# The last plain column group of an output projection in two parts, one ahead of seven products and one behind them

## The chip, the cores and the metric

The kernel runs on one core of a Trainium2 chip. The metric is device time in microseconds (us), the median of three runs. Engines are named as the profile names them: PE (TensorE matmul), PEld (its weight load), DVE (VectorE), ACT (ScalarE), POOL (GpSimd), SP (the engine that issues most DMAs; "SPq" is its queue). POOL issues DMAs of its own on a second queue.

## The reference

One encoder layer: 16 meta tokens and 512 real ones, width 2048, float32. Only the end matters here: two mixers of 1024 columns each are gated, put side by side and projected once; the result is normalised by row and added to the input.

```
ya = gqa_axial_mixer(...)  * silu(ga)        # mixer A, 8 heads of 128
yb = diff_attn_mixer(...)  * silu(gb)        # mixer B, 8 heads of 128
y  = concatenate([ya, yb]) @ w_out           # (tokens, 2048) x (2048, 2048)
h  = h + rmsnorm(y, post_norm_g)             # mean square over the 2048 columns
return h[:, N_META:, :]                      # 512 rows
```

The kernel splits every operand into a high part (rounded to float32r) and a low part (the rest), and multiplies in three matmuls: high x high, low x high, high x low.

## The kernel before, in words

**Rows, columns, contraction.** The output has four row blocks of 128 tokens (`t` = 0..3) and four column groups of 512 (`g` = 0..3). The contraction runs over 16 head blocks `j` of 128; the weights are laid out so that 0..7 are mixer B and 8..15 mixer A. `oh[j]`, `ol[j]` are the high and low parts of a head block; the unsplit heads lie in DRAM as `oscr`.

**Plain groups.** `dense_out(g)` computes one column group for all four row blocks: 16 head blocks x 4 row blocks x 3 matmuls = 192 matmuls of 128x512, into four PSUM banks.

**Seven products.** Groups 1 and 2 are computed together by a Strassen-like scheme over halves (row halves x contraction halves x the two groups): seven `product` calls of 48 matmuls in the place of eight. Two operands of the calls are sums: of weight blocks, kept in four tiles `ch0`..`ch3` ("chain") that are changed between calls, and of heads, `t1`..`t4`, each four pairs of high and low tiles. `u` tiles hold two of these in turn, `v` tiles the other two. A head sum is made from halves of `oscr` loaded into tiles `ts`, a DVE subtraction, the high part by ACT (`hi`, line 306) and the low part by DVE (`lo`, line 309).

**Weight blocks.** Weights of 128x1024 (two head blocks by 512 columns, 512 KB) pass through a list `todo` in the order of use. `fetch` keeps two ahead: DMA into `st` (3 buffers, SP queue, line 147), `wh` by ACT (line 154), `wl` by DVE (line 155), 3 buffers each. Numbered from the start of the projection, blocks 1 to 8 serve group 0 and 9 to 16 group 3; then each product takes four. A plain group's block feeds 24 matmuls, a product's 12. For chain blocks there is no `st`: `wh` and `wl` are split from `ch`.

**Order before.** Group 0, group 3 (whole), then products 1 to 7: heads B lower rows, heads A lower rows, t1, t2, heads A upper rows, t3, t4. Chain sums are made in part by a DMA that adds (on the POOL queue), in part by a load into `st` and a DVE addition (line 700). During group 3 `first_sums` loads three half heads per step and makes t1 and t2; `third_sum` and `fourth_sum` stand in products 4 and 6. Row blocks 2 and 3 are finished ahead of product 7; product 7 does its last three weight blocks row block by row block, and `end` finishes row blocks 0 and 1.

**What sets the order.** Within one engine instructions run in the order that the tile framework's scheduler gave them when the kernel was built, from its own model of durations; it moves loads and splits far ahead of where they stand in the code. Each engine and each DMA queue then waits in order: an instruction whose input is late holds up all behind it.

Of the kernel before, what the change touches and what calls it, by code (L numbers as in the profile page):

```python
# [10 lines left out]
F32 = mybir.dt.float32  # L11
# [97 lines left out]
def kernel(ctx: ExitStack, tc: tile.TileContext, xT, xn, xm, w_s, w_t, w_q, w_o,  # L109
# [581 lines left out]
    def summed(add=None, fresh=None):  # L691

        def step(i):
# [3 lines left out]
            if add:  # L697
# [9 lines left out]
    todo += whole(0) + whole(3) + plain(0, 0) + plain(0, 1) + summed((0, 0)) + summed((0, 1))  # L707
    todo += summed((1, 0), fresh=(0, 0)) + summed() + plain(1, 1)
# [57 lines left out]
    def dense_out(g, pool, beside=None):  # L766

        pss = [pool.tile([P, 512], F32, name="po", tag="pd") for _ in range(TT)]
        for j0 in range(0, KT, 2):
            wh, wl = fetch()  # L770
            for j in (j0, j0 + 1):
# [5 lines left out]
                c = slice((j - j0) * 512, (j - j0 + 1) * 512)  # L777
                for t in range(TT):
                    tq = slice(t * P, (t + 1) * P)
                    mm(pss[t], oh[j][:, tq], wh[:, c], start=(j == 0), stop=False)  # L780
                    mm(pss[t], ol[j][:, tq], wh[:, c], start=False, stop=False)
                    mm(pss[t], oh[j][:, tq], wl[:, c], start=False, stop=(j == KT - 1))
                    lanes.poll()
            if beside:
                beside(j0 // 2)
        return pss

    first = dense_out(0, pd)
# [9 lines left out]
    def heads_of(i, half, dma):  # L798

        t = yp.tile([P, 2, NP], F32, name="ts", tag="ts", bufs=6)  # L800
        dma.dma_start(out=t, in_=oscr[i].rearrange("i p q -> p i q")[:, :, half])
        return t
# [10 lines left out]
    t1, t2, t3, t4 = [], [], [], []  # L813

    def first_sums(i):
        b0, b1, a1 = [heads_of(j, half, nc.gpsimd)
                      for j, half in ((i, lo_), (i, hi_), (4 + i, hi_))]
        TTv(out=b0, in0=b1, in1=b0, op=SUB)
        t1.append(operand("u", i, b0))
        TTv(out=a1, in0=a1, in1=b0, op=SUB)  # L820
        t2.append(operand("v", i, a1))

    def first_chain(i):
        nc.gpsimd.dma_start(out=chain[i], in_=block(1, 0, i))
        nc.gpsimd.dma_start(out=chain[i], in_=block(1, 1, i), accum_op=ALU.add)

    def third_sum(i):
        b1, a1 = heads_of(i, hi_, nc.sync), heads_of(4 + i, hi_, nc.sync)
        TTv(out=a1, in0=a1, in1=b1, op=SUB)
        t3.append(operand("u", i, a1))  # L830

    def fourth_sum(i):
        a0 = heads_of(4 + i, lo_, nc.sync)
        TTv(out=a0, in0=t2[i][0].bitcast(F32), in1=a0, op=SUB)
        TTv(out=a0, in0=a0, in1=t2[i][1].bitcast(F32), op=ALU.add)
        t4.append(operand("v", i, a0))
# [7 lines left out]
    def square(t, g, src):  # L844
        jk = yp.tile([P, 512], F32, name="jko", tag="jko", bufs=1)
        at = (0, 1, 3, 2)[g]
        nc.scalar.activation(jk, src, AF.Square, accum_out=ssy[t][:, at:at + 1])
# [6 lines left out]
    def product(ops, pool, beside=None, done=None):  # L854
# [184 lines left out]
```

## Time and profile before

| | |
|---|---|
| median of 3 runs | 955.04 us (954.67 to 955.67) |
| the profiled execution's own time | 955.66 us |
| its span, first to last instruction | 953.9 us |
| mean granted TensorE clock | 0.99 of full |
| group 0 ends, group 3 ends, product 7 starts, last matmul starts | about 810, 854.7, 922.67, 940.65 us |

All times below are in the span of that one execution. In a row of a timeline the columns are start, duration, engine, line, operation, output and inputs, count, and in brackets how long the engine had been idle and what ended that wait. A DMA row's last number is the median time from issue to landing.

### The profile page before, as it was taken

To read this page: it belongs to the slowest core of one execution; us is meant where nothing else is said; L and a number is where in the kernel's file an instruction comes from. 1 tells how busy PE (TensorE), PEld (TensorE's weight loads), DVE (VectorE), ACT (ScalarE), POOL (GpSimd) and SP (SyncE) were. 2 spreads that over 40 slices of the span, in tenths; PEclk is the share of its full clock that TensorE was granted. 3 is DMA by queue.
4 is the path that set the end of the run, shared out by engine and by line. 5 is a ranking of instruction groups with operands and counts; after the bars stand their busy time and mean duration, and the time that the engine had idled before them with its cause. 6 is when DMAs were issued, how large, how long until landed. Compare 5 with 4: busy or idle time off the path is not lost.

```text
span 953.9 us, 14190 instructions
## 1 busy us (share of the span) xinstructions
PE 926.4 (97%) x5498; PEld 810.8 (85%) x5498; DVE 584.6 (61%) x974; ACT 482.0 (51%) x845; POOL 164.0 (17%) x250
## 2 busy tenths in 40 slices
PE   9999999999999999999999999998999999999983
PEld 8899898989989898998997888886888888888862
DVE  6386576757575574757554274447554662476996
ACT  6664655546464554746552254354555743245531
POOL 0001010101001010101201041226212123201054
PEclk9999999999999999999999999999999999999996
DMA  9742122222223222312223223211222346976785
GB/s 333 260 159 99 67 88 88 79 77 100 76 78 99 82 84 77 100 67 78 89 67 100 89 68 109 67 58 54 80 75 78 128 141 202 292 226 193 232 278 196
DMA packets 40611, 117.16 MB, mean 123 GB/s; under 512 B 4672, under 2 KB 9536, under 8 KB 40416
## 3 DMA queue, kind: packets, MB, share of 16 engines
q1 hardware_dynamic: 37072, 104.71, 33.2%
q0 software_dynamic: 3328, 11.54, 4.1%
q8 instruction: 43, 0.70, 0.3%
q14 instruction: 24, 0.20, 0.1%
q10 hardware_dynamic: 144, 0.01, 0.0%
HBM read 107.85 MB, written 8.39 MB: 122 GB/s over the span
## 4 chain that ended last, share of the span: by engine, by line
PE 84%; DVE 7%; DMA 2%; POOL 2%; ACT 2%; issue 1%; SPq 0%; DVEq 0%; POOLq 0%; ACTq 0%
PE pd L63 54%; PE po L63 14%; PE sc L63 6%; PE pv L63 5%; PE tr L66 5%; DVE wl L155 1%; DVE qn L578 1%; DMA st<-in_w_o_dram 1%; DVE y L939 1%; POOL qn L592 1%; DMA ch<-in_w_o_dram 1%; POOL ssh L241 1%; DMA xns<-in_xn_dram 1%; DMA xs<-in_xT_dram 1%; ACT qn L650 0%
## 5 line engine op out<-in xcount | busy, mean ns | idle before, releaser
L63 PE MATMUL pd<-xh,wh 128*128 128x264 f32 (+1 forms) x992 | 333.3, 336 | 0.0
L63 PE MATMUL pd<-xl,wh 128*128 128x264 f32 (+1 forms) x992 | 324.9, 327 | 0.4 <-DVE xl L180 0.4
L63 PE MATMUL pd<-xh,wl 128*128 128x264 f32 (+1 forms) x992 | 324.9, 328 | 0.4 <-DVE wl L155 0.4
L154 ACT ACTIVATE wh<-st 128x1024 fp32r<-128x1024 f32 (+2 forms) x135 | 139.8, 1038 | 208.3 <-PE pd L63 90.5
L155 DVE TENSOR_TENSOR wl<-st,wh 128x1024 fp32r<-128x1024 f32 (+2 forms) x135 | 161.7, 1198 | 98.9 <-ACT wh L154 97.7
L63 PEld LDWEIGHTS pd<-xh,wl 128*128 128x128 f32 x992 | 186.6, 188 | 17.8 <-DVE wl L155 0.7
L63 PEld LDWEIGHTS pd<-xh,wh 128*128 128x128 f32 x992 | 187.3, 189 | 12.9 <-ACT xh L179 0.2
L63 PEld LDWEIGHTS pd<-xl,wh 128*128 128x128 f32 x992 | 187.5, 189 | 12.0 <-DVE xl L180 0.6
L63 PE MATMUL po<-wh,ol 128*128 128x512 f32 x176 | 69.6, 396 | 0.9 <-DVE ol L309 0.9
L63 PE MATMUL po<-wh,oh 128*128 128x512 f32 x176 | 70.3, 400 | 0.0
L63 PE MATMUL po<-wl,oh 128*128 128x512 f32 x176 | 69.8, 397 | 0.0
L463 ACT ACTIVATE p<-p,mx 128x528 f32<-128x528 f32 x64 | 46.5, 728 | 34.2 <-POOL mx L460 34.0
L453 DVE CUSTOM_DVE_ANT_0 p<-sc,dist 128x528 f32<-128x528 f32 x64 | 44.9, 702 | 24.0 <-PE sc L63 23.5
L309 DVE TENSOR_TENSOR pl<-tr,ph 128x512 fp32r<-128x512 f32 x64 | 43.4, 688 | 16.2 <-ACT ph L306 15.0
L306 ACT ACTIVATE ph<-tr 128x512 fp32r<-128x512 f32 x64 | 37.6, 590 | 30.9 <-PE tr L66 30.6
L63 PE MATMUL pd<-wh,xh 128*128 128x512 f32 x128 | 52.2, 408 | 0.8 <-DVE vf L300 0.8
L66 PE MATMUL tr<-ident,p 128*128 128x128 f32 (+1 forms) x320 | 50.9, 273 | 1.7 <-DVE gA L558 0.9
L63 PE MATMUL pd<-wh,xl 128*128 128x512 f32 x128 | 50.6, 395 | 0.0
L63 PE MATMUL pd<-wl,xh 128*128 128x512 f32 x128 | 50.5, 395 | 0.0
L66 PEld LDWEIGHTS tr<-ident,p 128*128 128x128 f32 (+1 forms) x320 | 37.3, 132 | 13.4 <-DVE gA L558 1.6
L413 POOL TENSOR_SCALAR pm<-pm 32x256 fp32r<-32x256 f32 x32 | 20.1, 627 | 149.7 <-ACT pm L306 145.8
L460 POOL TENSOR_SCALAR mx<-mx 128x2 f32<-128x2 f32 x32 | 12.1, 377 | 196.0 <-DVE mx L453 196.0
(206 smaller groups left out, 1582.6 us busy)
## 6 DMA issues: line engine op xcount, KB each, us to landing
st<-in_w_t_dram SPq DMA_DIRECT2D x82, 512.0 KB, 3.6
st<-in_w_o_dram SPq DMA_DIRECT2D x40, 512.0 KB, 4.3
st<-in_w_q_dram SPq DMA_DIRECT2D x16, 512.0 KB, 3.6
xs<-in_xT_dram SPq DMA_DIRECT2D x16, 264.0 KB, 5.7
xns<-in_xn_dram SPq DMA_DIRECT2D x8, 512.0 KB, 5.3
ch<-in_w_o_dram POOLq DMA_DIRECT2D x8, 512.0 KB, 8.8
out_dram<-y SPq DMA_DIRECT2D x16, 256.0 KB, 2.3
os<-oscr SPq DMA_DIRECT2D x6, 512.0 KB, 3.6
```

Source lines behind the costliest of these rows:

```text
L63: self._add(self.nc.tensor.matmul(out, lhsT, rhs, start=start, stop=stop), us)
L66: self._add(self.nc.tensor.transpose(out, in_, ident), 0.109)
L154: nc.scalar.activation(wh[:, c], st[:, c], AF.Copy)
L155: nc.vector.tensor_tensor(out=wl[:, c], in0=st[:, c], in1=wh[:, c].bitcast(F32), op=ALU.subtract)
L241: nc.gpsimd.tensor_tensor(out=dst, in0=dst, in1=mhalf[:rows, :dst.shape[1]], op=ALU.pow)
L306: nc.scalar.activation(dst, src, AF.Copy)
L309: nc.vector.tensor_tensor(out=dst, in0=src, in1=h.bitcast(F32), op=ALU.subtract)
L413: nc.gpsimd.tensor_scalar(out=pm[32:64], in0=pm[0:32].bitcast(F32), scalar1=1.0, scalar2=1.0, op0=ALU.mult, op1=ALU.mult)
L453: nc.vector.tensor_tensor_reduce(out=two(p), in0=sc[:, :, :HALF], in1=two(dist[:, w0:w0 + NT]), scale=1.0, scalar=-3.0e38, op0=ALU.add, op ...
L460: nc.gpsimd.tensor_scalar(out=mx, in0=mx, scalar1=-0.125, scalar2=1.0, op0=ALU.mult, op1=ALU.mult)
L463: nc.scalar.activation(p2[m], p2[m], AF.Exp, scale=0.125, bias=mx[:, m:m + 1], accum_out=sm[:, m:m + 1])
L578: nc.vector.scalar_tensor_tensor(out=raw[:, i, :], in0=raw[:, i, :], scalar=ss[:rows, i:i + 1], in1=g[:rows], op0=ALU.mult, op1=ALU.mult)
```

## The change

Group 3 is cut by contraction: its mixer B half (head blocks 0..7, weight blocks 9 to 12) runs where the whole group ran, its mixer A half (96 matmuls, four weight blocks) runs behind the seven products, in the same four PSUM banks, which stay taken in between. The last three blocks of that half go row block by row block, and `finish` ends each of the four row blocks as it comes. The products are now heads B lower (blocks 13 to 16), heads A lower (17 to 20), t1, t2, heads A upper, t4, t3. The first and second head sums are made apart: `first_sum` in the B half of group 3, `second_sum` in product 1, `fourth_sum` in product 5, `third_sum` in product 6. The tiles `ts` go from 6 buffers to 2, beside 4 new ones named `r` that keep an unsplit sum for the second one. One of the three additions to the chain is moved from DVE to a DMA that adds, on the POOL queue.

```
-            if add:
+                nc.gpsimd.dma_start(out=chain[i], in_=block(*add, i), accum_op=ALU.add)
+            elif add:
...
-    todo += whole(0) + whole(3) + plain(0, 0) + plain(0, 1) + summed((0, 0)) + summed((0, 1))
-    todo += summed((1, 0), fresh=(0, 0)) + summed() + plain(1, 1)
+    todo += whole(0) + whole(3)[:4] + plain(0, 0) + plain(0, 1) + summed((0, 0)) + summed((0, 1))
+    todo += summed((1, 0), fresh=(0, 0)) + plain(1, 1) + summed() + whole(3)[4:]
...
+    def dense_out(g, pss, first=0, end=KT, tail=0, done=None, beside=None):
...
+        last = [fetch(len(todo)) for _ in range(tail // 2)] if tail else []
+        for t in range(TT):
+            for j in range(end - tail, end):
+                part(t, j, last[(j - end + tail) // 2])
+            if done:
+                done(t, pss[t])
...
+    def first_sum(i):
+        b0 = heads_of(i, lo_, nc.gpsimd, "r", 4)
+        b1 = heads_of(i, hi_, nc.gpsimd)
+        nc.gpsimd.dma_start(out=chain[i], in_=block(1, 0, i))
+        nc.gpsimd.dma_start(out=chain[i], in_=block(1, 1, i), accum_op=ALU.add)
         TTv(out=b0, in0=b1, in1=b0, op=SUB)
         t1.append(operand("u", i, b0))
...
+    def second_sum(i):
+        a1 = heads_of(4 + i, hi_, nc.gpsimd)
+        TTv(out=a1, in0=a1, in1=raw[i], op=SUB)
         t2.append(operand("v", i, a1))
...
+    third = banks(pd2)
+    dense_out(3, third, 0, NH, beside=first_sum)
...
+    for u, ps in enumerate(product(of_y(0, 0), second_sum)):
...
+    for u, ps in enumerate(product(of_y(1, 1), fourth_sum)):
...
+    for u, ps in enumerate(product(of_t(t4), third_sum)):
+        TTv(out=C(1, 0, u), in0=C(1, 0, u), in1=ps, op=SUB)
+    last = product(of_t(t3), lambda i: residual(i - 2, "u") if i > 1 else None)
...
+    def finish(t, ps):
+        collect(3, t, ps)
...
+        for c0, c1 in zip(cuts, cuts[1:]):
+            v, x = y[t][:, c0:c1], xr[t][c0 // 512][:, c0 % 512:c0 % 512 + c1 - c0]
+            if last and c1 == DM:
+                nc.scalar.activation(v, v, AF.Copy, scale=r)
+                TTp(out=v, in0=v, in1=x, op=ALU.add)
+            else:
+                nc.vector.scalar_tensor_tensor(out=v, in0=v, scalar=r, in1=x, op0=ALU.mult,
+                                               op1=ALU.add)
+            if c1 in ((256, 1024, 1536, 2048) if last else (1024, 2048)):
+                load(out[t * P:(t + 1) * P, sent:c1], y[t][:, sent:c1])
+                sent = c1
+
+    dense_out(3, third, NH, KT, 6, finish)
```

Three places of the built order matter for what follows. The first is DVE from the split of weight block 13 to that of block 14. Before, inside group 3 (818 and 820 are the first and second subtraction, 309 a low part):

```order
L155 TENSOR_TENSOR wl<-st,wh 128x1024 x2
L818 TENSOR_TENSOR ts<-ts 128x512
L820 TENSOR_TENSOR ts<-ts 128x512
L309 TENSOR_TENSOR ul_8400<-ts,uh_8399 128x512
L818 TENSOR_TENSOR ts<-ts 128x512
L309 TENSOR_TENSOR vl_8405<-ts,vh_8404 128x512
L820 TENSOR_TENSOR ts<-ts 128x512
L309 TENSOR_TENSOR ul_8476<-ts,uh_8475 128x512
L155 TENSOR_TENSOR wl<-st,wh 128x1024
```

The last row is block 14. Now, from just ahead of block 14 to block 15, which are both product 1's (840 is the second sum's subtraction, 850 and 851 the fourth's):

```order
L840 TENSOR_TENSOR ts<-ts,r 128x512
L155 TENSOR_TENSOR wl<-st,wh 128x1024
L309 TENSOR_TENSOR vl_8461<-ts,vh_8460 128x512
L840 TENSOR_TENSOR ts<-ts,r 128x512
L850 TENSOR_TENSOR r<-vh_8435,r 128x512
L850 TENSOR_TENSOR r<-vh_8460,r 128x512
L309 TENSOR_TENSOR vl_8486<-ts,vh_8485 128x512
L851 TENSOR_TENSOR r<-r,vl_8436 128x512
L840 TENSOR_TENSOR ts<-ts,r 128x512
L851 TENSOR_TENSOR r<-r,vl_8461 128x512
L155 TENSOR_TENSOR wl<-st,wh 128x1024
```

Block 14's split now stands behind the second sum of step 1 (first row), block 15's behind that of step 3 (ninth row). The second place is the POOL queue from its first DMA of the projection on. Before:

```order
L824 DMA ch_8214<-in_w_o_dram 128x1024
L824 DMA ch_8215<-in_w_o_dram 128x1024
L801 DMA ts<-oscr_78 128x2x256
L825 DMA ch_8214<-in_w_o_dram 128x1024
L825 DMA ch_8215<-in_w_o_dram 128x1024
L801 DMA ts<-oscr_78 128x2x256
```

Now, from step 2 of `first_sum` to the end of `second_sum` (832 is the plain load of a chain tile, 833 the DMA that adds; `oscr` 82 to 85 are the half heads of the second sum):

```order
L815 DMA ts<-oscr_80 128x2x256
L832 DMA ch_8216<-in_w_o_dram 128x1024
L815 DMA r<-oscr_81 128x2x256
L815 DMA ts<-oscr_81 128x2x256
L832 DMA ch_8217<-in_w_o_dram 128x1024
L833 DMA ch_8216<-in_w_o_dram 128x1024
L815 DMA ts<-oscr_82 128x2x256
L833 DMA ch_8217<-in_w_o_dram 128x1024
L815 DMA ts<-oscr_83 128x2x256
L815 DMA ts<-oscr_84 128x2x256
L815 DMA ts<-oscr_85 128x2x256
```

The half heads of the second sum stand behind all eight chain loads. Ahead of the rows shown stand `r` and `ts` of steps 0 and 1, the loads of `ch` 8214 and 8215 with their additions, and `r` of step 2. The first `ts` load waits for a count of PE instructions that is one higher than that for which the second `ts` load waited before. The third place is DVE from the last chain block of product 5 to the last block of product 6 (845 is the third sum, 926 takes product 5 out of PSUM); now:

```order
L309 TENSOR_TENSOR vl_8927<-ts,vh_8926 128x512
L155 TENSOR_TENSOR wl<-ch_8217,wh 128x1024
L155 TENSOR_TENSOR wl<-st,wh 128x1024
L845 TENSOR_TENSOR ts<-ts 128x512
L155 TENSOR_TENSOR wl<-st,wh 128x1024
L926 TENSOR_TENSOR y_8222<-po,y_8222 128x512
L309 TENSOR_TENSOR vl_8952<-ts,vh_8951 128x512
L926 TENSOR_TENSOR y_8223<-po,y_8223 128x512
L155 TENSOR_TENSOR wl<-st,wh 128x1024
L845 TENSOR_TENSOR ts<-ts 128x512
L155 TENSOR_TENSOR wl<-st,wh 128x1024
```

Before, the four third subtractions (line 829) stood among the splits of group 3's last blocks, with six `ts` buffers; now each stands ahead of a weight split of products 2, 5 and 6, and its second load waits on the SP queue for the low part of the sum before it, which frees one of the two `ts` buffers.

165 lines of the change are left out of this document (57 added, 108 removed).

## The prediction

> **What bounds it now.** I read the page first, then the last products by stage, then the waits of PE.
>
> ```profile
> span 953.9 us, 14190 instructions
> PE 926.4 (97%) x5498; PEld 810.8 (85%) x5498; DVE 584.6 (61%) x974; ACT 482.0 (51%) x845; POOL 164.0 (17%) x250
> ```
> ```profile
> 910.00:920.00 10.00, 9.16 (x40) 6.98 (x38) 9.03 (x8) 4.41 (x7) 5.37 (x5) 1.00 0.71 241
> 920.00:930.00 10.00, 8.31 (x34) 6.22 (x34) 10.00 (x20) 3.86 (x6) 6.16 (x10) 1.00 0.90 311
> 930.00:940.00 10.00, 7.21 (x21) 5.28 (x22) 8.13 (x11) 2.39 (x5) 4.93 (x6) 0.66 0.49 189
> ```
>
> Columns: stage, length, busy time of PE, PEld, DVE, ACT, POOL, then granted clock, DMA share, GB/s. PE bounds the kernel at 97%, except in products 6 and 7, where it starves beside a DVE that is busy all the time, and after the last matmul. The matmuls show how much is lost:
>
> ```profile
> 898.96 0.39 PE L63 MATMUL po<-wh,oh 128*128 128x512 f32 x1
> 910.16 0.40 PE L63 MATMUL po<-wh,uh 128*128 128x512 f32 x1
> 920.25 0.50 PE L63 MATMUL po<-wl,uh 128*128 128x512 f32 x1 [1.10 <-DVE wl L155]
> 922.67 0.39 PE L63 MATMUL po<-wh,vh 128*128 128x512 f32 x1
> 926.98 0.39 PE L63 MATMUL po<-wh,vl 128*128 128x512 f32 x1
> 932.75 0.79 PE L63 MATMUL po<-wh,vh 128*128 128x512 f32 x1 [3.09 <-ACT wh L154]
> 937.59 0.46 PE L63 MATMUL po<-wh,vl 128*128 128x512 f32 x1
> 940.65 0.39 PE L63 MATMUL po<-wl,vh 128*128 128x512 f32 x1
> ```
>
> Product 5 takes 910.16 - 898.96 = 11.2 us (2.80 per block). From 922.67 to 926.98 lie 19 matmuls at 0.227 us, so a product on sums takes 48 x 0.227 = 10.9. Product 6 took 12.5 (lost: 1.6), product 7 with its last matmul's end at 941.04 took 18.4 (lost: 7.5). **Lost: 9.1 us.** In that lie ten matmuls at 0.48 us (932.75 to 937.59), 2.6 lost to the halved clock. Behind the last matmul the span has 953.9 - 941.0 = **12.9 us**.
>
> **Part 1: the gain at the end.** The matmuls are the same number; without waits the last one would end at 941.0 - 9.1 = 931.9. The change takes away what starved products 6 and 7: their chain loads start a product earlier, four DVE additions of 1.26 us go, and half of the residual loads meet the slow half group (24 matmuls per block) instead of products. The four DMAs that add instead are issued in product 5 and needed in product 7, with all of product 6 (10.9) between; without that cover each costs what it is late. Behind the last matmul, before:
>
> ```profile
> 942.30 0.68 DVE L968 TENSOR_TENSOR y<-y,po 128x512 f32<-128x512 f32 x1
> 943.07 0.63 ACT L847 ACTIVATE jko<-y 128x512 f32<-128x512 f32 x1 [1.39 <-DVE y L968]
> 928.12 1.44 POOL L896 TENSOR_TENSOR y<-y,gpB 128x512 f32<-128x512 f32 x1 [3.24 <-ACT jko L847]
> 945.46 0.55 POOL L930 TENSOR_TENSOR ry<-ry,mhalf 128x1 f32<-128x1 f32 x1
> 946.04 3.08 DVE L939 SCALAR_TENSOR_TENSOR y<-y,ry,xr 128x512 f32<-128x512 f32 x3 [0.71 <-POOL ry L930]
> 931.71 18.69 SPq L139 DMA_DIRECT2D out_dram<-y  x16
> ```
> ```profile
> L700 DVE TENSOR_TENSOR ch<-ch,st 128x1024 f32<-128x1024 f32 x12 | 15.1, 1259 | 1.6 <-DMA ch<-in_w_o_dram 1.5
> L939 DVE SCALAR_TENSOR_TENSOR y<-y,ry,xr 128x512 f32<-128x512 f32 x14 | 12.2, 919 | 2.3 <-POOL ry L930 2.3
> ```
>
> Square to row factor took 946.04 - 943.07 = 3.0, and the last store left the queue at 950.40, 3.5 before the end. Now the square reads PSUM at once, without the subtraction: factor at +3.0 (the row block ahead, 18 matmuls x 0.23 = 4.2 us earlier, needs 4 x 0.92 on DVE and is out of its way by then). Two half and two whole row pieces: 3 x 0.92 = 2.8, done at +5.8; two stores queue, 0.7; +3.5. Sum **10.0, a gain of 2.9**. With row pieces at the 0.68 of a plain DVE row it is 9.3; with two pieces of the block ahead in the way, 11.8. Other moved work (square sums, POOL multiplies of 1.44 us beside the half group) hides behind its 22 us of matmuls; uncovered, one such multiply in front of a split costs 1.4.
>
> **Part 2: the loss in product 1.** Group 3's whole 45 us stood between first sums and products; now 22 do. Clock of the blocks and of DMA:
>
> ```profile
> 821.14 1.06 ACT L154 ACTIVATE wh<-st 128x1024 fp32r<-128x1024 f32 x1 [0.95 <-PE po L63]
> 843.59 1.06 ACT L154 ACTIVATE wh<-st 128x1024 fp32r<-128x1024 f32 x1 [1.24 <-PE po L63]
> ```
> ```profile
> 799.21 0.28 PE L63 MATMUL pv<-pl,vh 128*128 128x256 f32 x1
> ```
> ```profile
> DMA packets 2750, 9.99 MB, mean 285 GB/s; under 512 B 384, under 2 KB 384, under 8 KB 2617
> q0 software_dynamic: 1737, 6.00, 63.6%
> ```
> ```profile
> 799.60:834.60 35.00, 35.00 (x152) 28.19 (x151) 13.89 (x19) 9.93 (x18) 11.87 (x16) 1.00 0.96 285
> ```
>
> The two ACT rows are splits that start when blocks 10 and 14 leave PE: 22.45 / 4 = 5.61 per block. So block 12 ends at 832.4, product 1 starts there; block 14 starts 2.80 later, and its third matmul, the first to read `wl`, at 835.6; block 15's at 838.4.
>
> On DVE block 14's `wl` stands behind the second sum of step 1. Its load is the seventeenth of the POOL queue counted from the first `ts`, and the first `ts` waits for PE, I take it for the attention's last reads (799.2), so at 799.6. By then: nine half heads (2.36 MB), eight chain loads (4.19), 6.55 MB. Before, that queue (q0) moved 6.00 MB in the 35 us from 799.6, with DMA engines at 0.96 of their time: no room. 6.55 / 6.00 x 35 = 38.2: landed at T = 837.8. Bounds: 834.6 if it is as quick as the old queue's first 35 us; 840 if the SP queue takes more. I take 837.8, the row's own rate.
>
> From T on, DVE starts (one behind the other):
>
> ```profile
> 836.18 1.22 DVE L155 TENSOR_TENSOR wl<-st,wh 128x1024 fp32r<-128x1024 f32 x1
> 837.32 0.69 DVE L309 TENSOR_TENSOR vl<-ts,vh 128x512 fp32r<-128x512 f32 x1
> 837.92 0.68 DVE L818 TENSOR_TENSOR ts<-ts 128x512 f32<-128x512 f32 x1
> ```
> ```profile
> ts<-oscr POOLq DMA_DIRECT2D x3, 256.0 KB, 4.0
> ```
>
> 1.14 for a split, 0.60 for a half head. Block 14 ready at T + 1.9 = 839.7: PE waits 4.1. Then the low part (+0.6), which frees a `ts` buffer; only now goes the load of step 3, 4.0 as in the quiet row; its subtraction, one more of line 851 and block 15's split: T + 1.9 + 0.6 + 0.1 + 4.0 + 0.65 + 0.6 + 1.2 = T + 9.0 = 846.8, against 838.4. **Sum of both waits: 8.4** (5.2 to 10.6 by the bounds on T; it is T - 829.4). The next two blocks fit behind. Nothing covers these waits: all of PE stands behind them, and all later work moves with it.
>
> **Clock.** Two idle stretches of PE about as long stand in the trace:
>
> ```profile
> 651.03 0.59 PE L63 MATMUL sc<-kh,qh 128*128 128x264 f32 x1 [2.98 <-ACT p L550]
> ```
> ```profile
> 650.00:652.00 2.00, 0.97 (x4) 0.97 (x5) 0.92 (x3) 1.81 (x7) 0.81 (x2) 0.75 0.00 0
> 652.00:654.00 2.00, 2.00 (x8) 1.47 (x7) 1.71 (x6) 0.04 (x1) 1.48 (x4) 0.50 0.00 0
> 654.00:656.00 2.00, 2.00 (x10) 1.68 (x9) 1.20 (x5) 1.54 (x4) 0.49 (x2) 0.89 0.00 0
> ```
>
> After 2.98 idle the clock was 0.50 for about 3.4 us (650 to 656 adds up to 3.4 at half; 1.7 lost), after 3.09 as above 2.6 lost; after 1.1 nothing. Behind the first wait a slow block 14 only fills the second wait, which shrinks from 4.3 to some 2.2, between the cases. I take **1.0**, of 0 to 2.6.
>
> **Part 3: the loss in product 6.** With two `ts` buffers the third sums are a ring: load, subtraction, low part, next load. Three such loads L end in front of block 4 of product 6. DVE's list from product 5's start: the first load starts 2.8 ahead (there the low part ran before):
>
> ```profile
> 895.43 0.68 DVE L309 TENSOR_TENSOR vl<-ts,vh 128x512 fp32r<-128x512 f32 x1
> ```
> ```profile
> ts<-oscr SPq DMA_DIRECT2D x2, 256.0 KB, 3.3
> ```
> ```profile
> st<-in_w_o_dram SPq DMA_DIRECT2D x4, 512.0 KB, 5.0
> st<-in_w_o_dram SPq DMA_DIRECT2D x1, 512.0 KB, 8.8
> ```
>
> 895.43 + 0.68 is 2.85 before 898.96. Then L, 0.65, two splits and five half heads (5.3) to the low part; L, 0.65, a split and two half heads (2.35), L, 0.65 and 1.2: ready at 3 L + 8.0, needed at 11.2 + 3 x 2.73 + 0.46 = 19.9. The rows are the loads issued from 880 to 900, from 900 to 915 and from 915 to 925. With 3.3 for the quiet first load and 5.0 for the others, 13.3 + 8.0 = 21.3: **1.4 lost**. All at 3.3: nothing. Two at 8.8, as beside residual loads: 9.
>
> **Sum.** Last matmul 931.9 + 8.4 + 1.0 + 1.4 = 942.7, end +10.0 = 952.7, against 953.9: 1.2 less. This execution took 955.66 itself, 0.6 over the median; by difference, 955.0 - 1.2 = **953.9 us**. So the end's 9.1 + 2.9 are won, and 10.8 given back earlier.
>
> **Rivals.**
>
> *The second sums come in time.* For it: the old first sums stood on DVE in front of block 14 too and waited 6.66 us for their loads, and PE lost nothing:
>
> ```profile
> 830.12 0.69 DVE L818 TENSOR_TENSOR ts<-ts 128x512 f32<-128x512 f32 x1 [6.66 <-DMA ts<-oscr]
> ```
>
> Against: blocks then fed 24 matmuls. If T is 834 or less, product 1 loses 4 at most, no clock drop, product 6 nothing: 931.9 + 4 + 10 = 945.9, **about 947 us**.
>
> *The ring of third sums decides: slower.* In products 5 and 6 four chain loads, four adding DMAs, six half heads and weight blocks crowd into 20 us. For it: such crowds had 8.8 for a load. It decides from 3 L = 15 on (3.1 lost instead of 1.4, with which the gain is gone); at two loads of 8.8 the loss is 9 instead of 1.4, 952.7 + 7.6, **about 961**; half of that, 957 to 958. Against: the loads of 900 to 915, in the same traffic of chain and weights, had 5.0.
>
> *The clock halves after each wait.* Then 2.6 in product 1 and 1.7 behind product 6's wait come in place of 1.0: 952.7 + 3.3, **about 957**. For it: both idle stretches of about 3 us did it; against: the third wait is 1.4 and the second shortened. The Trainium skill, "TensorE: Matmul & The Clock Gate", Part 1, gives free-running windows of 3.4 us, the clock halved after an idle one; the trace agrees in the 3.4 us, but halved already after 2.98 idle, so by the rule only the first wait would surely count.
>
> **Chances.** My sum 0.48, its own range 950.5 to 957; in time 0.22; ring 0.22; clock 0.08. About 0.2% (1.9 us) can be told from no change. My sum lies inside that, with 0.20 of faster, 0.21 of same, 0.07 of slower; in time is faster; the ring is slower but for 0.03 same; the clock 0.04 same, 0.04 slower. Faster 0.42, same 0.28, slower 0.30. Range 946.5 to 960.5: from in time to the ring's bound, past which I leave a tenth on either side.
>
> **What would show it.** Product 1: PE waits on `wl` (line 155) of some 4 us twice, DVE idle ahead of line 840 for `ts` loads landing near 838; a wait under 1 refutes part 2. Product 6: one wait of 1 to 3 us ahead of its last block, behind line 845. Half clock within 10 us of 847. No wait in product 7 or the last half group, and 9 to 11 us behind the last matmul; a wait there refutes part 1. A weight block later than DVE is for the SP queue, held by `r` and `ts` loads, and would be outside all of this.

## The result and the profile after

The changed kernel takes 967.7 us (median; 964.2 to 970.4) against 955.3 us: **ratio 1.0126, interval 1.0101 to 1.015**. It is slower, and outside the range of 946.5 to 960.5. Of the cases told, the ring of third sums (about 961) comes nearest. The profiled execution took 965.27 us itself. From its page, and its table by stage (columns as in the prediction):

```profile
span 963.5 us, 14186 instructions
...
PE 928.8 (96%) x5498; PEld 812.3 (84%) x5498; DVE 577.2 (60%) x970; ACT 481.4 (50%) x844; POOL 165.9 (17%) x259
```
```profile
832.00:845.00 13.00, 8.24 (x27) 5.86 (x26) 6.92 (x10) 3.78 (x5) 1.46 (x2) 0.74 0.76 216
845.00:857.00 12.00, 8.46 (x25) 6.37 (x25) 9.54 (x12) 4.18 (x5) 0.00 (x0) 0.71 0.64 197
...
901.00:912.00 11.00, 7.13 (x31) 5.22 (x30) 5.64 (x6) 3.97 (x7) 4.31 (x4) 1.00 1.03 282
912.00:922.00 10.00, 6.66 (x29) 5.15 (x30) 5.70 (x7) 3.59 (x4) 5.20 (x9) 1.00 0.99 338
```

PE starves in two places: in product 1 (832 to 857, at a granted clock of 0.74 and 0.71) and in product 6 (901 to 922, full clock, DMA engines busy all the time). Products 2 to 5 and product 7 lose nothing, the half group 0.2. What PE waited for from 780 on (us in total, times, longest):

```profile
PE po L63 <- DVE wl L155: 13.2, 5, 3.5
PE po L63 <- ACT wh L154: 2.3, 1, 2.3
```

**Product 1.** PE's matmuls, then DVE's rows, then ACT's:

```profile
835.12 0.40 PE L63 MATMUL po<-wl,oh 128*128 128x512 f32 x1
837.85 0.50 PE L63 MATMUL po<-wh,oh 128*128 128x512 f32 x1 [2.33 <-ACT wh L154]
...
841.18 0.80 PE L63 MATMUL po<-wl,oh 128*128 128x512 f32 x1 [2.43 <-DVE wl L155]
...
849.53 0.79 PE L63 MATMUL po<-wl,oh 128*128 128x512 f32 x1 [3.54 <-DVE wl L155]
```
```profile
839.30 0.69 DVE L840 TENSOR_TENSOR ts<-ts,r 128x512 f32<-128x512 f32 x1 [1.72 <-DMA ts<-oscr]
839.91 1.22 DVE L155 TENSOR_TENSOR wl<-st,wh 128x1024 fp32r<-128x1024 f32 x1
...
847.05 0.69 DVE L840 TENSOR_TENSOR ts<-ts,r 128x512 f32<-128x512 f32 x1 [2.21 <-DMA ts<-oscr]
847.66 0.68 DVE L851 TENSOR_TENSOR r<-r,vl 128x512 f32<-128x512 f32 x1
848.26 1.22 DVE L155 TENSOR_TENSOR wl<-st,wh 128x1024 fp32r<-128x1024 f32 x1
```
```profile
836.22 0.63 ACT L306 ACTIVATE vh<-ts 128x512 fp32r<-128x512 f32 x1 [7.81 <-DVE ts L840]
836.76 1.04 ACT L154 ACTIVATE wh<-st 128x1024 fp32r<-128x1024 f32 x1
```

The splits of blocks 14 (839.91) and 15 (848.26) start behind second sums that wait for loads. On ACT the high part of block 14 (`wh`, 836.76) stands behind that of a second sum too. From 835.35 to 841.18 PE ran only two matmuls. Then it ran at half clock twice: 9 matmul spacings took 3.95 us (841.18 to 845.13) and 13 took 5.72 (849.53 to 855.25), where one takes 0.2326 at full clock. Product 1 ends at 857.38 after 24.8 us: **13.6 lost**, 9.0 in the three idle stretches and 4.6 at the halved clock.

**Product 6.** DVE's rows, PE's, and the DMAs issued from 895 to 900:

```profile
906.13 0.69 DVE L845 TENSOR_TENSOR ts<-ts 128x512 f32<-128x512 f32 x1 [6.88 <-DMA ts<-oscr]
906.74 1.22 DVE L155 TENSOR_TENSOR wl<-st,wh 128x1024 fp32r<-128x1024 f32 x1
...
916.30 0.69 DVE L845 TENSOR_TENSOR ts<-ts 128x512 f32<-128x512 f32 x1 [4.53 <-DMA ts<-oscr]
916.91 1.22 DVE L155 TENSOR_TENSOR wl<-st,wh 128x1024 fp32r<-128x1024 f32 x1
```
```profile
908.01 0.50 PE L63 MATMUL po<-wl,uh 128*128 128x512 f32 x1 [3.07 <-DVE wl L155]
...
911.82 0.50 PE L63 MATMUL po<-wl,uh 128*128 128x512 f32 x1 [0.79 <-DVE wl L155]
...
918.18 0.50 PE L63 MATMUL po<-wl,uh 128*128 128x512 f32 x1 [3.34 <-DVE wl L155]
```
```profile
ch<-in_w_o_dram POOLq DMA_DIRECT2D x1, 512.0 KB, 9.6
st<-in_w_o_dram SPq DMA_DIRECT2D x1, 512.0 KB, 10.4
ts<-oscr SPq DMA_DIRECT2D x1, 256.0 KB, 9.0
```

The splits behind the waits of 3.07 and 3.34 stand right behind a third sum (line 845). The loads of these two sums took 9.0 us (issued at 897.00) and 7.0 (at 909.18) to land, beside DMAs that add (`ch` on POOLq). The split behind the 0.79, at 909.67, took 2.09 us instead of 1.22, beside two multiplies of POOL. Product 6: 19.0 us, **8.1 lost**. Behind the last matmul:

```profile
953.65 0.39 PE L63 MATMUL po<-wl,oh 128*128 128x512 f32 x1
...
955.28 0.55 POOL L947 TENSOR_TENSOR ry<-ry,mhalf 128x1 f32<-128x1 f32 x1
...
955.86 3.27 DVE L957 SCALAR_TENSOR_TENSOR y<-y,ry,xr 128x256 f32<-128x256 f32 x4 [0.31 <-POOL ry L947]
```

Matmuls end at 954.04; the row factor is there 1.8 later, the row pieces at 959.13, the span ends at 963.5: **9.5** where it was 12.9.

### The profile page after: what moved, and what is told of

Same layout as the page of the kernel before. It is cut to its first block, busy times and chain, and to the rows that moved or that the text cites. A ratio compares the mean times of both kernels' runs of the same rounds, so it can differ in the third digit from the quotient of the medians.

```text
span 963.5 us, 14186 instructions
## 1 busy us (share of the span) xinstructions
PE 928.8 (96%) x5498; PEld 812.3 (84%) x5498; DVE 577.2 (60%) x970; ACT 481.4 (50%) x844; POOL 165.9 (17%) x259
## 5 line engine op out<-in xcount | busy, mean ns | idle before, releaser
L63 PEld LDWEIGHTS pd<-xl,wh 128*128 128x128 f32 x992 | 187.2, 189 | 11.4
L63 PE MATMUL po<-wl,oh 128*128 128x512 f32 x176 | 71.8, 408 | 6.0 <-DVE wl L155 6.0
L63 PEld LDWEIGHTS po<-wl,oh 128*128 128x128 f32 x176 | 34.3, 195 | 15.1 <-DVE wl L155 7.0
```

The lines of the kernel that those rows point to most:

```text
L63: self._add(self.nc.tensor.matmul(out, lhsT, rhs, start=start, stop=stop), us)
```

## Experiments

Theory after the result: two losses that don't depend on each other, one in product 1 from the place of the second sums, one in product 6 from third sums whose loads the adding DMAs slow. Rivals: too little matmul work in front, or the ring of two buffers by itself. A wider one came later: DVE and ACT work in order, so any load, sum or multiply that stands ahead of a weight split can stall PE, and each repair only shows the next such place.

"Lost" is the length of a product, from its first matmul to the next one's, less 11.2 (plain heads), 10.9 (sums), 22.4 (half group) or 16.8 (when three blocks stand behind). P1-3 are products 1 to 3, half is the half group behind product 7; each run also has the number by which the texts of what was expected call it. The losses are from one profiled execution each, which lies up to 4 us off the median. Product 6 differs between executions: it lost 13.3 and 13.6 in e3 and e8, which have the same order of instructions there as the changed kernel with its 8.1. So small differences of a loss prove little, and the medians have to bear them out.

| run | median us | ratio (95%) | P1-3 | P4-5 | P6 | P7 | half |
|---|---|---|---|---|---|---|---|
| before | 955.3 | 1 | 0 | 0 | 1.6 | 7.5 | - |
| after | 967.7 | 1.0126 (1.0101-1.015) | 13.6 | 0 | 8.1 | 0 | 0.2 |
| order (e1) | 962.4 | 1.0073 (1.0051-1.0096) | 3.2 | 0.4 | 14.2 | 0 | 0.3 |
| ring (e2) | 959.5 | 1.0044 (1.0023-1.0065) | 10.0 | 0 | 2.2 | 0 | 0.2 |
| fifth block in front (e3) | 963.1 | 1.0079 (1.0053-1.0104) | 7.9 | 0 | 13.3 | 0 | 0.2 |
| no late adding DMA (e4) | 960.9 | 1.0051 (1.0036-1.0067) | 9.9 | 3.2 | 3.8 | 0 | 0.2 |
| order + ring (e5) | 960.2 | 1.0053 (1.0033-1.0073) | 3.7 | 0.2 | 13.0 | 0 | 0.3 |
| order + ring, no late adding (e6) | 955.0 | 1.0006 (0.9997-1.0015) | 2.2 | 8.4 | 0.9 | 0 | 0.3 |
| plain for adding (e7) | 960.3 | 1.0056 (1.0039-1.0072) | 13.2 | 0 | 3.6 | 0 | 0.2 |
| first adding later (e8) | 968.9 | 1.015 (1.0132-1.0167) | 11.4 | 0 | 13.6 | 0 | 0.2 |
| all in code order (e9) | 956.7 | 1.0011 (0.9995-1.0027) | 4.3 | 0.2 | 3.8 | 2.9 | 0.3 |
| same, adding DMAs (e10) | 958.0 | 1.0028 (1.0014-1.0042) | 6.4 | 0.3 | 1.7 | 6.7 | 0.3 |
| spread (e11) | 953.7 | 0.9983 (0.9972-0.9994) | 5.9 | 0.1 | 4.5 | 0 | 0.2 |
| spread, no late adding (e12) | 955.8 | 0.9999 (0.9986-1.0011) | 5.5 | 0.1 | 4.7 | 2.5 | 0.2 |
| even (e13) | 952.6 | 0.9972 (0.9961-0.9982) | 1.2 | 0.3 | 4.1 | 0 | 4.5 |
| even, fifth block (e14) | 958.4 | 1.0034 (1.002-1.0047) | 0.6 | 0.3 | 4.7 | 0 | 9.5 |
| even, fifth block, own tiles (e15) | 954.9 | 0.9995 (0.9985-1.0006) | 0.6 | 0.3 | 2.0 | 0 | 8.7 |
| even, own tiles, late multiply (e16) | 946.0 | 0.9913 (0.9899-0.9926) | 0.6 | 0.3 | 1.8 | 0 | 0.2 |
| before, code order (e17) | 967.7 | 1.014 (1.0123-1.0156) | 0 | 5.1 | 5.8 | 9.3 | - |

### Product 1: order, work in front, the POOL queue

Order: the splits (`a` is the high part on ACT, `b` the low part on DVE) and the second sums with their two parts keep the order of the code.

```
+            if rank[0] == 40:
+                tc.keep_in_program_order(a)
+                tc.keep_in_program_order(b)
...
+        tc.keep_in_program_order(TTv(out=a1, in0=a1, in1=raw[i], op=SUB))
```


> Edit of the changed kernel: the weight splits of the products and the second sums keep, on DVE and on ACT, the order of the program text, so that the splits of blocks 14 and 15 stand ahead of the first second sum, and one split between every two sums. No load is moved. Theory of the queue behind the sum: product 1 lost 13.6 us (24.8 instead of 11.2) only because splits stood behind sums whose loads land at 835.5, 839.3 and 847.0. Then PE waits in product 1 fall from 8.3 us in three waits to under 1 us, no half clock there, although the loads land as late as before; product 6 loses its 8 us as before; time 952 to 955 (967.7 - 13.6). Rival, the DMA engines: they ran at 0.96 of their time from 800 to 835, so the weight blocks themselves are late, or the wait comes back in products 2 to 4, which need the sums: product 1 to 4 together lose more than 6 us, time above 960.

Product 1 lost nothing, and 2.8 came back in product 2, so most of the 13.6 was the place of the second sums. But product 6 lost 14.2, with one wait of 12.13 (PE at 908.11), and the time stayed above the expected 952 to 955. DVE's third sum, and the DMAs issued from 885 to 890:

```profile
906.23 0.69 DVE L851 TENSOR_TENSOR ts<-ts 128x512 f32<-128x512 f32 x1 [15.46 <-DMA ts<-oscr]
```
```profile
ch<-in_w_o_dram POOLq DMA_DIRECT2D x3, 512.0 KB, 12.0
...
ts<-oscr SPq DMA_DIRECT2D x2, 256.0 KB, 16.9
```

Three adding DMAs ran together, and the loads of 256 KB issued beside them took 16.9 (median of two).

Fifth block in front: `whole(3)[:5]` ahead of the products, three blocks behind.

```
-    dense_out(3, third, 0, NH, beside=first_sum)
+    dense_out(3, third, 0, NH + 2, beside=lambda i: first_sum(i) if i < 4 else None)
```


> Edit of the changed kernel: five instead of four weight blocks of group 3 stand in front of product 1, three instead of four behind product 7; the order of DVE in product 1 is the same. Product 1 starts 5.6 us later, at about 838.1. If T, the landing of the load of the second sum of step 1, is set by the POOL queue alone, it stays at 839.2: no wait ahead of block 14, 4 us ahead of block 15, one drop of the clock at most: product 1 loses 4 to 6.6 us instead of 13.6, time 958 to 961. If T is set by what PE frees (loads move along with the work), it moves by up to 5.6 us and product 1 still loses more than 10 us, time 965 or above.

5.6 us more of matmuls in front took 5.7 from product 1 (13.6 to 7.9). In the profiled execution product 6, with `ts` loads of 11.5 us (median of two), gave it back. The time came out 2 us above the first of the two expectations.

First adding later: the first chain's adding DMAs behind the second sums' loads in the POOL queue.

```
     def first_sum(i):
...
-        nc.gpsimd.dma_start(out=chain[i], in_=block(1, 1, i), accum_op=ALU.add)
...
     def second_sum(i):
         a1 = heads_of(4 + i, hi_, nc.gpsimd)
+        nc.gpsimd.dma_start(out=chain[i], in_=block(1, 1, i), accum_op=ALU.add)
```


> Edit of the changed kernel: the first four adding DMAs (for the chain of product 3) are issued behind the second sums' loads in the program, so the POOL queue has two of them instead of four (and no wait for a plain chain load) ahead of the load of step 1. DVE's order stays. If T is set by what stands ahead in the POOL queue, that load lands by 832 instead of 839, PE waits in product 1 under 3 us instead of 8.3, time 955 to 960. If the DMA engines' bytes alone set it (they were busy 0.96 of the time), T stays at 837 or later, product 1 loses 10 us or more, time 964 to 968.

```profile
827.89 0.69 DVE L840 TENSOR_TENSOR ts<-ts,r 128x512 f32<-128x512 f32 x1 [4.19 <-DMA ts<-oscr]
...
837.80 0.69 DVE L850 TENSOR_TENSOR r<-vh,r 128x512 f32<-128x512 f32 x1 [2.84 <-DMA r<-oscr]
838.41 0.69 DVE L840 TENSOR_TENSOR ts<-ts,r 128x512 f32<-128x512 f32 x1
839.01 0.69 DVE L851 TENSOR_TENSOR r<-r,vl 128x512 f32<-128x512 f32 x1
839.61 1.22 DVE L155 TENSOR_TENSOR wl<-st,wh 128x1024 fp32r<-128x1024 f32 x1
```

The second sum of step 1 came at 827.89 instead of 839.30: the order of the POOL queue sets T, as the prediction had it. Yet block 14's split stayed at 839.61. The scheduler had changed DVE's order, which the expectation took as fixed: the split now stands behind fourth sums (line 850) that wait for `r`. An earlier load bought nothing, since the next late load stood in front of the same split, and the time lies outside both expectations.

### Product 6: the ring and the adding DMAs

Ring: the third sum's second half head goes to the four `r` tiles.

```
-        b1, a1 = heads_of(i, hi_, nc.sync), heads_of(4 + i, hi_, nc.sync)
+        b1, a1 = heads_of(i, hi_, nc.sync), heads_of(4 + i, hi_, nc.sync, "r", 4)
```


> Edit of the changed kernel: one of the two loads of each third sum goes to the tiles r (four buffers, free by then), so that the ring of two ts tiles takes only the other load and is freed by the subtraction, not by the low part. Bytes and sums stay. Theory of the ring: product 6 lost 8.1 us (19.0 instead of 10.9) because three loads of 3.4, 9.0 and 7.0 us ran one after the other between DVE steps; with loads started earlier and side by side the PE waits of product 6 (7.6 us in three waits) fall to under 2 us, time about 960 (967.7 - 8). Rival, the crowd: loads are slow in 890 to 912 whatever starts them (DMA engines at 0.98 to 1.03 of their time), so a sum stays late and product 6 loses 4 us or more, time 963 or above. Product 1 as before in both (13.6 lost).

No late adding DMA: the four additions to the chain in product 5 go back to a load into `st` and DVE.

```
-                nc.gpsimd.dma_start(out=chain[i], in_=block(*add, i), accum_op=ALU.add)
+                st = wp.tile([P, 1024], F32, name="st", tag="st")
+                nc.sync.dma_start(out=st, in_=block(*add, i))
+                nc.vector.tensor_tensor(out=chain[i], in0=chain[i], in1=st, op=ALU.add)
```


> Edit of the changed kernel: the four additions to the chain that were moved to adding DMAs go back to a load into st (SP queue) and an addition on DVE. If the adding DMAs (7.7 to 9.6 us each, four of them from 893 to 917) made the loads of the third sums slow (9.0 and 7.0 us, 3.4 before them), these fall to 5 us or less and product 6 loses about 2 us instead of 8; DVE pays 5 us, partly in its idle time; time 960 to 965. If the bytes are what counts (the same 512 KB are loaded four times), the loads stay at 7 to 9 us, product 6 loses 7 to 11 us, time 967 to 972.

Plain for adding: the same bytes on the same queue; the addition is left out, so product 7 multiplies other weights.

```
-                nc.gpsimd.dma_start(out=chain[i], in_=block(*add, i), accum_op=ALU.add)
+                nc.gpsimd.dma_start(out=chain[i], in_=block(*add, i))
```


> Edit of the changed kernel: the four adding DMAs between products 5 and 7 become plain loads of the same bytes to the same tiles from the same queue; the sum is left out, so product 7 multiplies other weights and takes as long. If it is the adding that slows the loads beside it, the loads of the third sums take 5 us or less (9.0 and 7.0 with adding), product 6 loses at most 3 us instead of 8, time 960 to 963. If 2 MB more on another queue at that time are enough, they still take 7 us or more and the time stays 965 to 968.

Product 6 lost 2.2, 3.8 and 3.6 instead of 8.1; without the late adding DMAs product 5 lost 3.2 besides. Without these DMAs, the third sum's load issued from 890 to 895; with plain DMAs in their place, DVE's third sums:

```profile
ts<-oscr SPq DMA_DIRECT2D x1, 256.0 KB, 4.0
```
```profile
902.46 0.69 DVE L845 TENSOR_TENSOR ts<-ts 128x512 f32<-128x512 f32 x1 [3.74 <-DMA ts<-oscr]
...
904.81 0.68 DVE L309 TENSOR_TENSOR vl<-ts,vh 128x512 fp32r<-128x512 f32 x1
...
911.44 0.69 DVE L845 TENSOR_TENSOR ts<-ts 128x512 f32<-128x512 f32 x1 [3.23 <-DMA ts<-oscr]
```

From the end of the low part (905.49) to the next sum (911.44) lie 5.95. So the ring loads take 4.0 without the late adding DMAs, 5.9 and 5.8 beside plain ones, 9.0 and 7.0 beside adding ones. The run with plain DMAs differs in the adding alone: it accounts for some 4.5 of the 8.1 here, and by the medians for 7.4 of 967.7. It needs the ring: without the ring 5.9 of the 8.1 are gone though the DMAs still add. In the ring run's profile (955.7, the quickest of its executions, 955.7 to 963.8) the second sum of step 1 came at 836.70 with its place in the code unchanged: T differs by 2.6 between executions, which is the larger part of the 3.6 that its product 1 lost less.

### Repairs together

The order and the ring (edits as above), then without the late adding DMAs as well:

> The edits of e1_order1 and e2_ring3 together: splits in front of the second sums, and the third sums' loads no longer one after the other. If the two losses add up and come away apart, product 1 loses 1 us and product 6 2 us (as in e1 and e2 each), time 967.7 - 12.5 - 6 = 949 (947 to 952). Rival: the loads of the third sums take as long as the adding DMAs beside them run (16.9 us in e1, where these stood together at 884 to 895), so that starting them earlier only moves the wait: product 6 loses 6 us or more, time 955 or above.

> The edits of e1_order1, e2_ring3 and e4_no_dma_add together: no adding DMAs behind product 3, four additions of 1.2 us back on DVE. If the three causes are the whole loss (13.6 + 8.1), product 1 loses 1 us, product 6 0 to 3, the end stays: 967.7 - 12.5 - 6.5 = 948.7, 944 to 950, faster than the kernel before by 0.6 to 1.2%. Rival: the additions and their loads through the three st buffers hold up the weight blocks of product 6 (e4 had a wait of 3.0 us there behind wh): products 5 and 6 lose 6 us or more, time 953 or above.

Both times lie above what was expected. With both, product 6 lost 13.0 to a third sum that waited 11.96 for its load (16.6 from issue to landing, beside three adding DMAs). Without those, product 5 lost 8.3, its split now behind an addition that waits for a chain load (PE waited 5.12 at 888.04, and the clock halved):

```profile
885.62 1.23 DVE L702 TENSOR_TENSOR ch<-ch,st 128x1024 f32<-128x1024 f32 x1 [1.62 <-DMA ch<-in_w_o_dram]
886.77 3.49 DVE L155 TENSOR_TENSOR wl<-ch,wh 128x1024 fp32r<-128x1024 f32 x3
```

Here the theory of two independent losses fell: each repair moved the wait to the next place where something stands ahead of a split. What follows sets that order by hand.

### The order set by hand

All in code order: splits, sums and additions; fourth sums in product 2, third sums in product 6, with or without adding DMAs.

```
+    def in_p1(i):
+        if i:
+            second_sum(i - 1)
+
+    def in_p2(i):
+        if i == 0:
+            second_sum(3)
+            fourth_sum(0)
+        elif i == 1:
+            fourth_sum(1)
...
-    for u, ps in enumerate(product(of_y(1, 1), fourth_sum)):
+    for u, ps in enumerate(product(of_y(1, 1), add_chain)):
```


> Edit of the changed kernel: all that was found so far, in one. Splits, all later head sums and the chain additions of product 5 keep the order of the program on DVE and ACT; second sums stand one block later, fourth sums in product 2, third sums in product 6 behind the splits fetched by then, one of their loads in the tiles r; no adding DMAs behind product 3, their four additions on DVE in product 5, each with its own load into st just ahead. If a split behind a sum (or behind an addition, as in e6 in product 5: 5.1 us) is the whole of the loss, products 1, 5 and 6 together lose 3 us or less (after: 21.7), the last matmul ends at 932 to 936, the end takes 9.4 more: time 943 to 948, 0.8 to 1.2% faster than the kernel before. Rival: DVE and the three st buffers are too full in products 5 to 7 (four splits, four sums, four additions and eight updates are some 33 us of work in 33 us), so the wait comes back there: 6 us or more lost, time 951 or above.

> As e9_best, but the four additions of product 5 are done by adding DMAs again, as in the changed kernel. If the place of the splits decides and not the time of the loads, it loses as little as e9_best (3 us or less), time 943 to 948. If the adding DMAs slow every load beside them (16.9 us for a half head and 14.7 for a weight block in e1), weight blocks of product 6 come late themselves, whatever the order on DVE: product 6 loses 5 us or more behind wh or wl, time 949 or above, and 4 us or more over e9_best.

Both times lie above what the theory gave: no long wait is left, but many of up to 2.5 us in products 2, 3, 6 and 7. With the adding DMAs product 6 lost only 1.7, but product 7 lost 6.7: there a third sum whose load took 11.5 stood ahead of a split's high part on ACT, for which PE waited 2.20 at 913.66.

Spread: fourth sums a block earlier, the eight multiplies by the norm's weight on POOL behind product 7, and the loads of the residual kept in the order of the code. With the late adding DMAs the third sums stand in product 5 (shown); without them they stay in product 6.

```
+    def in_p1(i):
+        if i:
+            second_sum(i - 1)
+        if i > 1:
+            fourth_sum(i - 2)
...
+    def add_chain(i):
+        nc.gpsimd.dma_start(out=chain[i], in_=block(1, 0, i), accum_op=ALU.add)
+        if i < 3:
+            third_sum(i)
```


> From e10_best_dma_add, three moves that take DVE work out of the products where e9 and e10 still waited: fourth sums one weight block earlier (into the idle time of products 1 and 2), third sums in product 5 (their loads then land before the adding DMAs start), and all eight multiplies by the norm weight on POOL behind product 7, since DVE rows of 0.68 us took 1.7 to 3.8 us beside them (in e9 at 856, in e10 at 900). If a full DVE is what is left (4.3 us lost in product 3, 1.7 in product 6, 6.6 in product 7 of e10), products 3, 6 and 7 lose 3 us or less together and the time is 944 to 949. Rival: the adding DMAs, now beside the weight loads of products 6 and 7 alone, still make these late (10 us and more in e1): 5 us or more lost behind wh there, time 951 or above.

> From e9_best, two of the same moves: fourth sums one weight block earlier, the eight multiplies on POOL behind product 7. The additions stay on DVE in product 5, the third sums in product 6. If POOL's multiplies caused product 3's loss (4.3 us) it goes; products 6 and 7 (3.8 and 2.9 lost behind st loads that wait for a buffer held by an addition) keep 4 to 6; time 949 to 952. If product 3's wait is DVE's own amount of work, it stays: 955 to 957.

The first lies 4.7 us above its range, with 5.0 lost in product 2. There DVE has two sums for one block: a chain of 4.46 us, in which it waits 0.70 for ACT, for 2.80 of matmuls. In the second run product 3 lost 0.8 instead of 4.3, as expected of the multiplies, but product 2 lost 4.6, and the time stayed at that of the kernel before.

Even: one head sum per block in products 1 and 2, four of the eight multiplies on DVE behind product 7, the other four on POOL at their old place, and the residual's loads left to the scheduler; then with a fifth block in front; then with the first halves of third sums 2 and 3 loaded into their own `vl` tiles.

```
+    def in_p1(i):
+        (second_sum, second_sum, fourth_sum, second_sum)[i]((0, 1, 0, 2)[i])
+
+    def in_p2(i):
+        (fourth_sum, second_sum, fourth_sum, fourth_sum)[i]((1, 3, 2, 3)[i])
...
+            b1 = yp.tile([P, 2, NP], F32R, name=f"vl{i}", tag=f"vl{i}").bitcast(F32)
```


> From e11_spread_dma_add: in products 1 and 2 one head sum per weight block (second sums 0 and 1, fourth 0, second 2, fourth 1, second 3, fourth 2 and 3) instead of a second and a fourth sum in the same block, and the four early multiplies by the norm weight on DVE behind product 7 instead of POOL. In e11 a block of product 2 cost DVE a chain of 4.46 us (sum, high part on ACT, low part, fourth sum, split) where PE needs 2.80, 5.0 lost in all. If that uneven order is what is left of the loss there, products 1 to 3 lose 2.5 us or less together (5.8 in e11), time 949 to 952. If DVE has too much to do there in any order, since 22 us of PE work no longer stand in front, they lose 4 us or more, time 952 to 955.

> As e13_even_front4, with five weight blocks of group 3 in front of product 1 and three behind product 7 (5.6 us of PE work moved back to the front). If the missing PE work in front is what makes DVE too full in products 1 to 3, these lose 1 us or less and 2 us less than in e13, time 947 to 950. If e13 loses nothing there already, the fifth block brings nothing (within 1 us of e13).

> As e14_even_front5, with the first halves of third sums 2 and 3 loaded into the tiles that will hold their low parts, instead of into the ring of two ts tiles, so that all loads of the third sums are issued before or with the first adding DMA. Product 6 lost 4.5 us in e11 (a ts load of 8.6 us beside the adding DMAs, a split behind it, and a half clock of ten matmuls). If that load is the cause, product 6 loses 2 us or less, 2.5 less than e14. If the weight loads beside the adding DMAs are the cause, it stays at 4 to 5.

Products 1 to 3 lost 1.2 as expected, and 0.6 with a fifth block, so work in front is not what lacks. The half group lost 4.5 and 9.5, which no expectation had, and which put both times above what was expected (by 0.6 and 8.4): DVE's multiplies stood ahead of the last splits, and beside POOL's own the four took 6.3. DVE, then POOL, with the fifth block:

```profile
922.63 6.34 DVE L929 TENSOR_TENSOR y<-y,gpB 128x512 f32<-128x512 f32 x4
...
929.54 1.22 DVE L157 TENSOR_TENSOR wl<-st,wh 128x1024 fp32r<-128x1024 f32 x1
```
```profile
922.12 6.31 POOL L929 TENSOR_TENSOR y<-y,gpB 128x512 f32<-128x512 f32 x4
```

Own tiles took product 6 from 4.7 to 2.0, as expected. The last version is the even one with four blocks in front, own tiles, and the multiplies behind the last splits:

```
         last = [fetch(len(todo)) for _ in range(tail // 2)] if tail else []
+        if done:
+            for t in range(TT):
+                scale(0, t // 2, t % 2)
```


> As in the run with four blocks in front and even head sums, with two edits: the first halves of third sums 2 and 3 are loaded into tiles of their own, and the four early multiplies stand behind the splits of the last half group and no more ahead of the last one. Theory (a sum, a load or a multiply costs PE time only where it stands ahead of a weight split that PE needs): the half group loses at most 0.5 where it lost 4.5, product 6 at most 2 where it lost 4.1, products 1 to 3 as there (1.2); matmuls end near 936, and with 9.5 to 10 behind them 945 to 948 us. Rival (the traffic of the adding DMAs slows the weights of products 6 and 7 wherever the sums stand): 4 or more lost there, 950 us or more.

```profile
915.97 2.08 DVE L157 TENSOR_TENSOR wl<-st,wh 128x1024 fp32r<-128x1024 f32 x1 [0.61 <-ACT wh L156]
918.47 1.82 DVE L157 TENSOR_TENSOR wl<-st,wh 128x1024 fp32r<-128x1024 f32 x1 [0.41 <-ACT wh L156]
920.22 2.48 DVE L937 TENSOR_TENSOR y<-y,gpB 128x512 f32<-128x512 f32 x4
```
```profile
r<-oscr SPq DMA_DIRECT2D x1, 256.0 KB, 10.0
```

**945.99 us, 0.9913 (0.9899 to 0.9926) of the kernel before**, in the expected range: 2.9 lost in all. The second fence is a load issued from 880 to 890: it is as slow as ever beside an adding DMA, but no row of DVE waits for it. So the theory of places holds for this order, and the adding DMAs cost little where nothing that PE needs stands behind a late load.

Last, the kernel before with its splits in code order (the first edit above alone):

> The kernel before, with one edit: the weight splits of the projection keep their order of the code on ACT and DVE. Theory (the gain of the last versions is from the half group behind the products and the even sums, the order alone has nothing to give the old arrangement, whose loss in product 7 is from DVE being busy all the time): within 0.4% of the kernel before, 951 to 959 us. Rival (the order alone was the trouble there too): product 7's 7.5 us fall to 4 or less, 951 us or less.

Neither expectation came true: 967.7 us, 1.4% slower. PE's longest wait, 7.41 at 944.44, is for the first of the two splits in the second row, which stand behind eight row pieces:

```profile
936.86 6.39 DVE L942 SCALAR_TENSOR_TENSOR y<-y,ry,xr 128x512 f32<-128x512 f32 x8 [2.47 <-POOL ry L933]
943.17 2.35 DVE L155 TENSOR_TENSOR wl<-st,wh 128x1024 fp32r<-128x1024 f32 x2
```

The order of the code is no better in itself; here too, work for rows that nobody waits for stood ahead of a split. Whether the old arrangement could gain as much with its order set by hand was not tried.

## Why the prediction was wrong, point by point

In the span, 952.7 was forecast and 963.5 measured. The difference of 10.8 is product 1 +4.2, product 6 +6.7, the end without waits +0.4 (954.04 - 13.6 - 8.1 = 932.3 against 931.9), the tail -0.5.

- **Part 1, the gain at the end: right.** No wait in product 7 (7.5 lost before) or the half group, and none in product 6 that comes from the chain. The tail came to 9.5 against 10.0: the factor was ready at +1.8, not +3.0, the row pieces at +5.1 against +5.8, and 4.4 followed instead of 4.2.
- **Part 2, product 1: mechanism right, three sizes off.** The sums and loads ahead of the splits were those named (the order run removed the loss from product 1, the later adding moved T by 11.4). T was 839.3 instead of 837.8 (+1.5); the load of step 3 took 5.0 (issued at 842.03), not 4.0 (+1.0); the clock cost 2.7 beyond what the second wait hid, not 1.0 (+1.7). They add up to the 4.2. Not seen was that ACT's high part of block 14 stands behind a second sum's as well (2.33); it only came in front of waits that were there anyway.
- **Part 3, product 6: the step that failed.** "With 3.3 for the quiet first load and 5.0 for the others": the others took **9.0 and 7.0**. 3.4 + 9.0 + 7.0 = 19.4, and by the prediction's own formula 19.4 + 8.0 - 19.9 = 7.5 lost, measured 8.1. The 5.0 was from loads beside plain traffic, while here four DMAs that add ran in a row and took 7.7 to 9.6 us each. What a load on the SP queue takes beside such DMAs stood in the trace of before, and the sum did not use it. There two adding DMAs, issued at 817.92 and 818.96, and five `ts` loads ran on the POOL queue beside these two weight loads, issued from 820 to 825 (so the row does not price the adding alone):

```profile
ts<-oscr POOLq DMA_DIRECT2D x5, 256.0 KB, 12.0
st<-in_w_o_dram SPq DMA_DIRECT2D x2, 512.0 KB, 9.0
```

The rival had the 8.8 that came nearest, and I gave it 0.22, arguing that the traffic was the same as before. It was not: the plain run shows 5.9 for the same bytes. Part of the size is one execution's: product 6 lost 13.3 and 13.6 in e3 and e8, with the same order there.
- **The clock.** It halved twice in product 1 and not after the 3.07 and 3.34 of product 6, so the rival that gave it after each wait is wrong as well. The length of a wait alone does not tell it. The granted clock fell at 838.24 and 848.48 and rose at 845.07 and 855.31, and these times lie a whole number of steps of 3.41 us apart. Cut into such steps, the two ahead of the falls and one of product 6 are (columns as in the table by stage):

```profile
834.83:838.24 3.41, 1.08 (x5) 0.50 (x4) 1.39 (x2) 1.57 (x2) 0.36 (x1) 1.00 0.85 226
845.07:848.48 3.41, 0.92 (x4) 0.40 (x3) 1.43 (x3) 0.70 (x2) 0.00 (x0) 1.00 0.49 172
...
913.33:916.74 3.41, 1.51 (x7) 0.93 (x5) 0.44 (x1) 0.00 (x0) 2.80 (x6) 1.00 1.02 334
```

PE idled 2.3 and 2.5 us of the first two steps, and the clock fell at their ends. Each wait of product 6 lies across two steps; PE idled at most 1.9 us of any one of them, and the clock stayed. In the other traces, from 640 us on, every fall follows a step with 1.8 us idle or more, and every step at full clock with more than 2.0 us idle is followed by one. The Trainium skill, "TensorE: Matmul & The Clock Gate", Part 1, has free-running windows of 3.4 us and halves the clock after an idle one: the steps agree, but in neither window here was PE idle throughout, and the measurement decides.

The range was too low because its ends came from the bounds of single terms, and both large terms moved up together; the 961 of the ring has product 1 at its middle value.

## What to carry to other kernels

On an engine that takes its instructions in order, ask of each operand PE needs what stands ahead of it, and price that with its latest load; a load made earlier helps only if it was the last late thing ahead of that split. A load time is to be taken from a row with the same kind of traffic beside it, not only the same bytes. Once the pieces are known, spread them one to a block and put work that nobody waits for behind the splits: here that was worth 2.2% between two arrangements of the same matmuls (967.7 and 946.0).

## What the hardware showed unexpectedly

- A DMA that adds (512 KB, POOL queue) took 6.8 to 12.8 us from issue to landing behind product 4, over all runs. Loads of 256 KB issued on the other queue while one ran took 4.8 to 18.0, against 3.2 to 4.1 without them (e4) and 4.8 to 5.9 beside plain DMAs of the same bytes (e7). The Trainium skill, "DMA: Bandwidth & Descriptors", "Anatomy of one DMA", fits 2.0 us + bytes / 436e3 to a DMA from that queue, an estimate of 3.2 for these. No adding one of any run came near it (5.3 at least), but neither did the plain ones from that queue (4.1 at least), and none ran alone.
- Two-input operations of DVE stretch beside those of POOL: from 0.62 to 1.58 for a multiply (2.48 and 6.34 for four), from 1.22 to 2.08 for a split (in the last version, where POOL's four ran from 913.17 to 919.21). "GPSIMD Engine Reference", section 1, of the Trainium skill names this contention; the rows agree.
- The clock stayed at half for 6.8 us both times in product 1 (838.24 to 845.07 and 848.48 to 855.31): two steps of 3.41 each time, and in the first of the two PE still idled (2.4 and 1.0 us).
